# The last per-layer input of a two-layer trunk: half of its feature blocks for all tokens, half of them by halves of the tokens with weights split once

## The chip, the cores and the metric

The kernel runs on one core of a Trainium2 chip. The metric is the device time of one execution in microseconds (us), the median of several runs. A change under 0.2% (about 4.6 us here) can't be told from no change.

## The reference, cut to what matters

The trunk has two layers (DEPTH = 2) over 512 tokens of 1024 features, all in f32. What the change touches is the last step of each layer, the per-layer input embedding (PLE), in the second layer, and the final norm behind it:

```python
for i in range(DEPTH):
    ...                                   # FFN, conv + attention mixer, FFN
    gate = jax.nn.sigmoid(rmsnorm(h, ple_norm[i]) @ w_ple_gate[i])   # 1024 -> 1024
    h = h + gate * (p[i] @ w_ple_proj[i])                            # 256 -> 1024
return rmsnorm(h, final_norm)
```

`rmsnorm` divides by the root of the mean square over the 1024 features of a token, and multiplies by a gain per feature.

## The kernel before

Activations are held with features on the partitions: `h` is 8 tiles (feature blocks) of 128 features x 512 tokens. Every matrix product is made of three matmuls per 128x128 weight tile (`mm3`, lines 198 to 200): the f32 operands are split into a high part (rounded to fp32r) and a low part (the rest), and high x high, high x low and low x high are added up in PSUM.

Weights come through `Stream W`: halves of 8 tiles (128 x 1024 f32, 512 KB) are loaded by SP's DMA queue (line 51) into a pool of ten raw buffers, and `split` (lines 67 and 68) makes the high part with a copy on ACT and the low part with a subtraction on DVE, both 1024 columns wide, into rotating buffers `wh` and `wl` (four of each). `W.get` hands out the next tile. A weight that is needed twice is loaded and split twice. Other tiles of 128 x 512 come from one pool `G` of N_BIG = 58 buffers.

`ple` first splits the scaled `h` (`normed`) and `p`. A feature block m needs 8 gate tiles and 2 projection tiles, 10 x 3 matmuls. `rms` is made of two matmuls with ones (`e1ps`) and a chain on ACT and DVE: Sqrt, a reciprocal of 3.35 us, and three more DVE operations. `ple_add` then does, per block: multiply by r (line 781, DVE), Sigmoid (782, ACT), multiply by the projection (783, DVE), add to `h` (784, DVE).

In layer 0 (`halves` false) a block is one pass over 512 tokens (tiles `e0gp`, `e0pp`). In the last layer (`halves` true) all 8 blocks are done for tokens 0 to 255, then all 8 for tokens 256 to 511 (tile `e1gp`, 256 columns for the gate and 256 for the projection), and each half has an object `Final`:

- `add(k)`: square `h[k]` on ACT and add it to an accumulator on DVE (`facc`, line 259; the last two blocks stay apart as `fsq`); for the last three blocks two matmuls with a column of ones each (tile `fss`, line 808); and scale `h[k]` by the final gain on DVE (`fh`, line 811);
- `turn(kk)`: transpose four feature blocks back to tokens on the partitions, 4 transposes per 128 tokens (tile `ft`, line 819); for kk = 0 the result is copied to SBUF by ACT (`fu`, line 822);
- `finish`: the factor per token (`fr`, lines 830 to 837, with a Sqrt on ACT), four scalings (`fo`, lines 842 and 844), and four output DMAs (line 846).

The list `late` holds these steps back: up to 6 of them stay behind the blocks in the first half, 3 in the second. So the first half's `turn(0)`, `add(5)`, `add(6)` and `add(7)` are issued behind block 0 of the second half. The framework's scheduler orders the instructions of each engine at build time: the written order is the priority, and an instruction that it thinks is not ready can be passed by a later one. On the chip each engine runs its list strictly in order.

Of the kernel before, what the change touches and what calls it, by code (L numbers as in the profile page):

```python
# [24 lines left out]
SCALE = float((NOPE + ROPE) ** -0.5)  # L25
TWO_PI_PARTS = (6.28125, 0.001922607421875, 1.2695789337158203e-05, 3.958120942115784e-09, 1.0231815394945443e-11)

N_BIG = 58
N_RAW = 10
N_WH = 4  # L30

# [1 line left out]
class Stream:  # L33
# [64 lines left out]
    def halves_of(self, *tiles):  # L98

        h, l = self.get(*tiles)  # L100
        h3, l3 = (a.rearrange("p (k c) -> p k c", c=P) for a in (h, l))
        self.nc.scalar.copy(l3[:, :, :P // 2], h3[:, :, :P // 2].bitcast(F32))
        self.nc.gpsimd.memset(h3[:, :, P // 2:].bitcast(F32), 0.0)  # L103
        return l, h

    def col(self, name, l, c, rows, r0=0):

# [51 lines left out]
def trunk_kernel(ctx, tc, dims, x, p, positions, gains, rope_c, weights, out):  # L159
# [16 lines left out]
    def G(name, dt=F32):  # L176
        return gp.tile([P, S], dt, tag="g", name=name)

    def PS(name):
        return mp.tile([P, 512], F32, tag="mm", name=name)  # L180
# [21 lines left out]
    def proj(tiles, vs, name, ps=None):  # L202
        ps = PS(name) if ps is None else ps
        o = ps[:, :vs[0][0].shape[1]]
        for k, (t, v) in enumerate(zip(tiles, vs)):
            mm3(o, W.get(t), v, k == 0, k == len(tiles) - 1)
        return ps
# [30 lines left out]
    def gain(nm, l, k):  # L238
        c = col_at[nm, l] + k
        return cols[:, c:c + 1]  # L240
# [4 lines left out]
    class Squares:  # L245


        def __init__(self, name):
            self.name, self.acc = name, None

        def add(self, t):
            w = t.shape[1]
            if self.acc is None:
                self.acc = G(self.name + "acc")[:, :w]
                nc.scalar.activation(self.acc, t, AF.Square)
                return
            sq = G(self.name + "sq")[:, :w]
            nc.scalar.activation(sq, t, AF.Square)
            nc.vector.tensor_tensor(self.acc, self.acc, sq, ALU.add)
# [4 lines left out]
    def rms(acc, n, name, scale=1.0):  # L264

        ah, al = acc
        ps = PS(name + "ps")
        nc.tensor.matmul(ps, ones, ah, start=True, stop=False)
        nc.tensor.matmul(ps, ones, al, start=False, stop=True)
        r, t, ms = (rp.tile([P, S], F32, tag=g, name=name + w) for g, w in (("r", "r"), ("w", "t"), ("w", "ms")))  # L270
        nc.vector.tensor_scalar(ms, ps, 1.0 / n, EPS, ALU.mult, ALU.add)
        nc.scalar.activation(t, ms, AF.Sqrt)  # L272
        nc.vector.reciprocal(r, t)
        nc.vector.tensor_tensor(t, r, r, ALU.mult)
        nc.vector.scalar_tensor_tensor(t, t, -0.5 * scale, ms, ALU.mult, ALU.mult)
        nc.vector.scalar_tensor_tensor(r, t, 1.5 * scale, r, ALU.add, ALU.mult)
        return r
# [456 lines left out]
            nc.vector.tensor_tensor(h[m], ps, h[m], ALU.add)  # L734


    def ple(l, halves):

        name = f"e{l}"
        pt = []  # L740
        for k in range(PD // P):
            t = G(f"{name}pi{k}")
            nc.sync.dma_start(out=t, in_=p[l, k * P:(k + 1) * P, :])
            pt.append(split(t, f"{name}p{k}"))
        xs, acc = normed("ple", l, name)
        r = None
        late = []
        for toks in ((slice(0, S // 2), slice(S // 2, S)) if halves else (slice(0, S),)):
            pss = []
            final = Final(toks) if halves else None  # L750
            xt, ptt = ([(hi[:, toks], lo[:, toks]) for hi, lo in v] for v in (xs, pt))
            w = toks.stop - toks.start
            for m in range(KD):
                n = f"{m}_{toks.start}"
                pg = PS(f"{name}gp{n}")
                pp = pg[:, w:] if halves else PS(f"{name}pp{n}")
                pg = pg[:, :w]
                proj(W.col("w_ple_gate", l, m * P, D), xt, None, pg)
                proj(W.col("w_ple_proj", l, m * P, PD), ptt, None, pp)
                pss.append((pg, pp))  # L760
                if r is None and m == (2 if halves else 1):
                    r = rms(acc, D, name)
                    for mm in range(m):
                        ple_add(f"{name}{mm}_", mm, r, *pss[mm], toks)
                if r is not None:
                    ple_add(name + n, m, r, pg, pp, toks)
                if halves:
                    late.append(lambda f=final, m=m: f.add(m))
                    if m == KD // 2:
                        late.append(lambda f=final: f.turn(0))  # L770
                    if m == KD - 1:
                        late += [lambda f=final: f.turn(1), final.finish]
                    while len(late) > (3 if toks.start else 6):
                        late.pop(0)()
        for step in late:
            step()

    def ple_add(name, m, r, pg, pp, toks):
        w = toks.stop - toks.start
        g = rp.tile([P, S], F32, tag="w", name=f"{name}g{m}")[:, :w]  # L780
        nc.vector.tensor_tensor(g, pg, r[:, toks], ALU.mult)
        nc.scalar.activation(g, g, AF.Sigmoid)
        nc.vector.tensor_tensor(g, pp, g, ALU.mult)
        nc.vector.tensor_tensor(h[m][:, toks], h[m][:, toks], g, ALU.add)


    class Final:
        def __init__(self, toks):
            self.t0, self.w = toks.start, toks.stop - toks.start
            self.toks, self.nt = toks, (toks.stop - toks.start) // P  # L790
            self.sq = Squares(f"f{toks.start}")
            self.hg, self.turned = [], {}

        def add(self, k):
            n = f"{k}_{self.t0}"
            hk = h[k][:, self.toks]
            if k < KD - 2:
                self.sq.add(hk)
                sq = self.sq.acc
            else:  # L800
                sq = G("fsq" + n)
                nc.scalar.activation(sq[:, :self.w], hk, AF.Square)
            part = k - (KD - 3)
            if part == 0:
                self.ss = PS(f"fss{self.t0}")
            for t in range(self.nt if part >= 0 else 0):
                c = 4 * part + t
                nc.tensor.matmul(self.ss[:, c:c + 1], sq[:, t * P:(t + 1) * P], ones[:, 0:1].bitcast(F32),
                                 start=True, stop=True)
            hg = G("fh" + n)  # L810
            nc.vector.tensor_scalar(hg[:, :self.w], hk, gain("final", 0, k), None, ALU.mult)
            self.hg.append(hg)

        def turn(self, kk):
            for t in range(self.nt):
                n = f"{t}_{kk}_{self.t0}"
                ps = PS("ft" + n)
                for c in range(4):
                    nc.tensor.transpose(ps[:, c * P:(c + 1) * P], self.hg[4 * kk + c][:, t * P:(t + 1) * P], ident)
                if 4 * kk + 4 < KD:  # L820
                    o = G("fu" + n)
                    nc.scalar.copy(o, ps)
                    ps = o
                self.turned[t, kk] = ps

        def finish(self):
            nt = self.nt
            fr = cp.tile([P, 16], F32, tag=f"fr{self.t0}", name=f"fr{self.t0}")
            ms, rt, r, t_ = (fr[:, 4 * i:4 * i + nt] for i in range(4))
            nc.vector.tensor_scalar(ms, self.ss[:, :nt], 1.0 / D, EPS, ALU.mult, ALU.add)  # L830
            for c in (4, 8):
                nc.vector.scalar_tensor_tensor(ms, self.ss[:, c:c + nt], 1.0 / D, ms, ALU.mult, ALU.add)
            nc.scalar.activation(rt, ms, AF.Sqrt)
            nc.vector.reciprocal(r, rt)
            nc.vector.tensor_tensor(t_, r, r, ALU.mult)
            nc.vector.scalar_tensor_tensor(t_, t_, -0.5, ms, ALU.mult, ALU.mult)
            nc.vector.scalar_tensor_tensor(r, t_, 1.5, r, ALU.add, ALU.mult)
            for kk in range(KD // 4):
                for t in range(nt):
                    o = G(f"fo{self.t0}_{t}_{kk}")  # L840
                    if t % 2 == 0:
                        nc.scalar.activation(o, self.turned[t, kk], AF.Copy, scale=r[:, t:t + 1])
                    else:
                        nc.vector.tensor_scalar(o, self.turned[t, kk], r[:, t:t + 1], None, ALU.mult)
                    row = self.t0 + t * P
                    nc.sync.dma_start(out=out[row:row + P, kk * 512:(kk + 1) * 512], in_=o)

    for l in range(DEPTH):
# [52 lines left out]
```

## Time and profile before

| | us |
|---|---|
| median of 3 runs | 2320.2 (2319.61 to 2320.4) |
| the profiled execution's own time | 2319.08 |
| its span in the trace | 2317.3 |
| TensorE (PE) busy | 2294.0 (99%) |
| VectorE (DVE) busy | 1791.4 (77%) |
| ScalarE (ACT) busy | 1064.2 (46%) |

Times in rows are microseconds from the span's start, if they aren't marked ns. In a timeline row the columns are start, duration, engine, line, operation, output <- input, shapes, count, and in brackets the idle time of the engine before it with what ended it. Rows with a count above 1 merge neighbours. PEclk is the granted TensorE clock as a share of 2.4 GHz. A matmul's duration overlaps with the next one's; the step from start to start is what it costs.

### The profile page before, as it was taken

How to read it: one execution, taken by the hardware profiler on the slowest of the kernel's cores; microseconds unless marked ns; L12 is line 12 of the kernel's file. 1: busy time of each engine (PE TensorE's matmuls, PEld its weight loads, DVE VectorE, ACT ScalarE, POOL GpSimd, SP SyncE). 2: the span in 40 equal slices, each digit the busy share in tenths (PEclk: the TensorE clock that was granted, in tenths of full speed). 3: DMA queues.
4: the chain of work that ended last, by engine and by line, in shares of the span. 5: the costliest groups of instructions: out<-in, count | busy, mean ns of one | idle time of the engine just before them, and what ended most of it. 6: DMA issues, size and time to landing. Idle time of an engine off the chain costs nothing.

```text
span 2317.3 us, 33585 instructions
## 1 busy us (share of the span) xinstructions
PE 2294.0 (99%) x13696; PEld 2051.2 (89%) x13696; DVE 1791.4 (77%) x2483; ACT 1064.2 (46%) x1563; POOL 59.5 (3%) x58
## 2 busy tenths in 40 slices
PE   9999999999999999999999999999999999999997
PEld 7999988888888999998899999888888889999987
DVE  8988779745866988877898787687378679888776
ACT  7444444234544644444564444433245355444455
POOL 0000000200100000000000000001001000000000
PEclk9999999999999999999999999999999999999998
DMA  5333233332122233333223333322321213233341
GB/s 192 112 107 107 94 123 109 100 99 93 37 71 84 74 112 99 109 108 129 73 83 110 102 100 119 119 91 100 101 82 37 82 55 114 98 108 107 120 137 38
DMA packets 64523, 227.94 MB, mean 98 GB/s; under 512 B 7408, under 2 KB 7408, under 8 KB 64368
## 3 DMA queue, kind: packets, MB, share of 16 engines
q1 hardware_dynamic: 63936, 225.47, 29.7%
q8 instruction: 107, 1.75, 0.3%
q14 instruction: 48, 0.39, 0.1%
q10 hardware_dynamic: 432, 0.32, 0.0%
HBM read 223.66 MB, written 2.10 MB: 97 GB/s over the span
## 4 chain that ended last, share of the span: by engine, by line
PE 94%; DVE 4%; ACT 1%; issue 1%; DMA 0%; ACTq 0%; SPq 0%
PE a1pd L198 2%; PE b0pd L198 2%; PE b1pd L198 2%; PE a0pd L198 2%; PE b1pd L199 2%; PE b0pd L199 2%; PE a0pd L199 2%; PE a1pd L199 2%; PE a0pd L200 2%; PE a1pd L200 2%; PE b1pd L200 2%; PE b0pd L200 2%; DVE wl L68 1%; PE e1gp L198 1%; PE e1gp L199 1%; PE e1gp L200 1%
## 5 line engine op out<-in xcount | busy, mean ns | idle before, releaser
L67 ACT CAST wh<-st 128x1024 fp32r<-128x1024 f32 (+1 forms) x463 | 482.6, 1043 | 683.7 <-issue 146.3
L68 DVE TENSOR_TENSOR wl<-st,wh 128x1024 fp32r<-128x1024 f32 (+1 forms) x463 | 568.8, 1229 | 168.9 <-ACT wh L67 167.4
L67 ACT CAST wh<-s 128x1024 fp32r<-128x1024 f32 x78 | 81.9, 1050 | 101.0 <-PE b1pd L199 8.5
L68 DVE TENSOR_TENSOR wl<-s,wh 128x1024 fp32r<-128x1024 f32 x78 | 94.9, 1216 | 0.9 <-ACT wh L67 0.9
L135 DVE TENSOR_TENSOR st<-st,s 128x1024 f32<-128x1024 f32 x39 | 47.7, 1222 | 1.0
L138 DVE TENSOR_TENSOR st<-st,st 128x1024 f32<-128x1024 f32 x39 | 47.5, 1217 | 0.1
L132 DVE TENSOR_TENSOR s<-s,st 128x1024 f32<-128x1024 f32 x39 | 47.5, 1218 | 0.0
L127 DVE TENSOR_TENSOR s<-st,st 128x1024 f32<-128x1024 f32 x39 | 47.4, 1216 | 0.1
L469 DVE SCALAR_TENSOR_TENSOR h<-b0pd,h 128x512 f32<-128x512 f32 x40 | 27.5, 688 | 9.1 <-PE b0pd L200 9.1
L469 DVE SCALAR_TENSOR_TENSOR h<-b1pd,h 128x512 f32<-128x512 f32 x40 | 27.5, 688 | 9.1 <-PE b1pd L200 9.1
L469 DVE SCALAR_TENSOR_TENSOR h<-a1pd,h 128x512 f32<-128x512 f32 x40 | 27.5, 687 | 7.1 <-PE a1pd L200 7.0
L469 DVE SCALAR_TENSOR_TENSOR h<-a0pd,h 128x512 f32<-128x512 f32 x40 | 27.5, 687 | 6.4 <-PE a0pd L200 6.4
L103 POOL MEMSET wh<- 128x256 f32 x4 | 1.1, 312 | 1196.0 <-DVE wl L68 1196.0
L603 DVE TENSOR_TENSOR m1gm<-m1gmp,m1r 128x512 f32<-128x512 f32 x8 | 5.5, 691 | 26.5 <-PE m1gmp L200 26.5
L603 DVE TENSOR_TENSOR m0gm<-m0gmp,m0r 128x512 f32<-128x512 f32 x8 | 5.5, 691 | 26.2 <-PE m0gmp L200 26.2
L595 DVE TENSOR_TENSOR m1gc<-m1gcp,m1r 128x512 f32<-128x512 f32 x8 | 5.4, 689 | 11.3 <-PE m1gcp L200 11.3
L595 DVE TENSOR_TENSOR m0gc<-m0gcp,m0r 128x512 f32<-128x512 f32 x8 | 5.4, 689 | 11.3 <-PE m0gcp L200 11.3
L598 DVE TENSOR_TENSOR m0gc<-m0cop,m0gc 128x512 f32<-128x512 f32 x8 | 5.4, 690 | 8.4 <-PE m0cop L200 8.3
L598 DVE TENSOR_TENSOR m1gc<-m1cop,m1gc 128x512 f32<-128x512 f32 x8 | 5.4, 691 | 8.4 <-PE m1cop L200 8.3
L729 DVE TENSOR_TENSOR m1gm<-m1mop,m1gm 128x512 f32<-128x512 f32 x8 | 5.5, 690 | 6.6 <-PE m1mop L200 6.5
L729 DVE TENSOR_TENSOR m0gm<-m0mop,m0gm 128x512 f32<-128x512 f32 x8 | 5.5, 690 | 6.6 <-PE m0mop L200 6.5
L272 ACT ACT_TABLE_LOAD x8 | 10.3, 1283 | 0.1
(10023 smaller groups left out, 8593.3 us busy)
## 6 DMA issues: line engine op xcount, KB each, us to landing
st<-in_weights SPq DMA_DIRECT2D x416, 512.0 KB, 3.5
st<-in_weights SPq DMA_DIRECT2D x8, 256.0 KB, 5.3
h<-in_x SPq DMA_DIRECT2D x8, 256.0 KB, 5.4
out<-fo SPq DMA_DIRECT2D x8, 256.0 KB, 2.3
e0pi<-in_p SPq DMA_DIRECT2D x2, 256.0 KB, 3.7
e1pi<-in_p SPq DMA_DIRECT2D x2, 256.0 KB, 3.8
pos_i<-in_positions ACTq DMA_DIRECT2D x1, 256.0 KB, 4.4
cols<-in_gains ACTq DMA_DIRECT2D x1, 53.0 KB, 3.0
```

What stands on the lines that cost most here:

```text
L67: self.nc.scalar.copy(hi[:, w], src[:, w])
L68: self.nc.vector.tensor_tensor(lo[:, w], src[:, w], hi[:, w].bitcast(F32), ALU.subtract)
L127: tt(self.s, self.a21, self.a22, ALU.add)
L132: tt(self.s, self.s, self.a11, ALU.subtract)
L135: tt(self.a12, self.a12, self.s, ALU.subtract)
L138: tt(self.a11, self.a11, self.a21, ALU.subtract)
L198: nc.tensor.matmul(ps, wh, vh, start=first, stop=False)
L199: nc.tensor.matmul(ps, wh, vl, start=False, stop=False)
L200: nc.tensor.matmul(ps, wl, vh, start=False, stop=last)
L469: nc.vector.scalar_tensor_tensor(h[m], ps, 0.5, h[m], ALU.mult, ALU.add)
L603: nc.vector.tensor_tensor(g, ps, r, ALU.mult)
L729: nc.vector.tensor_tensor(t, mla_ps[m], t, ALU.mult)
```

## The change

In the last layer, `ple(l, last)`:

- feature blocks 0 to 3 are done for all 512 tokens at once, as layer 0 does;
- blocks 4 to 7 are done for tokens 0 to 255 and then for tokens 256 to 511, and their 40 weight tiles are loaded and split once (`W.kept`, 8 tiles at a time, in pieces of 512 columns) into 20 buffers of `G`, which stay until the end; three of the five `keep()` calls are issued with blocks 1 to 3, two with the first half's blocks 4 and 5;
- `rms` is issued behind block 1 (before: behind block 2);
- `Final` is one object for all tokens. `add` follows each `ple_add` at once, for the columns that it got; its scaling by the final gain goes from DVE to ACT. `sums`, `turn` and `finish` are calls of their own, for a half i or a block t of 128 tokens. `turn(t, 0)` of all four token blocks is issued in the first half (behind blocks 5 and 6); `sums(0, .)`, `turn(0, 1)`, `turn(1, 1)` and `finish(0)` behind blocks 4 and 5 of the second half; the rest behind the last block;
- N_BIG goes from 58 to 60, and the weight array no longer holds the last layer's PLE weights twice.

```diff
-N_BIG = 58
+N_BIG = 60
...
+    def kept(self, tiles, buffer):
+        res = []
+        st = self.raw(tiles)
+        for c in range(0, P * len(tiles), 512):
+            hi, lo = buffer(f"kh{c}", F32R), buffer(f"kl{c}", F32R)
+            self.nc.scalar.copy(hi, st[:, c:c + 512])
+            self.nc.vector.tensor_tensor(lo, st[:, c:c + 512], hi.bitcast(F32), ALU.subtract)
+            res += [(hi[:, w:w + P], lo[:, w:w + P]) for w in range(0, 512, P)]
+        return res
...
+        pss = []
+        n = (D + PD) // P
+        m0 = KD // 2 if last else KD
+        final = Final() if last else None
...
+        kept = sum((tiles(m) for m in range(m0, KD)), [])
+        ws = []
+        def keep():
+            ws.extend(W.kept([kept.pop(0) for _ in range(8)], G))
+        for m in range(m0):
+            if last and m >= 1:
+                keep()
+            pg, pp = PS(f"{name}gp{m}"), PS(f"{name}pp{m}")
+            for ps, vs, ts in ((pg, xs, tiles(m)[:KD]), (pp, pt, tiles(m)[KD:])):
+                proj(ts, vs, None, ps)
+            pss.append((pg, pp))
+            if m == 1:
+                r = rms(acc, D, name)
+                ple_add(f"{name}0_", 0, r, *pss[0], slice(0, S))
+                if last:
+                    final.add(0, slice(0, S))
+            if m >= 1:
+                ple_add(name, m, r, pg, pp, slice(0, S))
+                if last:
+                    final.add(m, slice(0, S))
...
+        for i in range(2):
+            toks = slice(i * (S // 2), (i + 1) * (S // 2))
+            for m in range(m0, KD):
+                if kept:
+                    keep()
+                ps = PS(f"{name}gp{m}_{i}")
+                pg, pp = ps[:, :S // 2], ps[:, S // 2:]
+                for j, (hi, lo) in enumerate(xs + pt):
+                    o, first, end = (pg, j == 0, j == KD - 1) if j < KD else (pp, j == KD, j == n - 1)
+                    mm3(o, ws[(m - m0) * n + j], (hi[:, toks], lo[:, toks]), first, end)
+                ple_add(f"{name}{i}", m, r, pg, pp, toks)
+                final.add(m, toks)
+                if i == 0 and m - m0 in (1, 2):
+                    for t in (0, 1) if m - m0 == 1 else (2, 3):
+                        final.turn(t, 0)
+                if i == 1 and m == m0:
+                    final.sums(0, KD - 3)
+                if i == 1 and m == m0 + 1:
+                    final.sums(0, KD - 2)
+                    final.sums(0, KD - 1)
+                    final.turn(0, 1)
+                    final.turn(1, 1)
+                    final.finish(0)
+        final.sums(1, KD - 3)
+        final.sums(1, KD - 2)
+        final.turn(2, 1)
+        final.sums(1, KD - 1)
+        final.turn(3, 1)
+        final.finish(1)
...
+        def add(self, k, toks):
+            hk = h[k][:, toks]
+            if k == 0:
+                nc.scalar.activation(self.acc[:, toks], hk, AF.Square)
             else:
-                sq = G("fsq" + n)
-                nc.scalar.activation(sq[:, :self.w], hk, AF.Square)
+                sq = self.sq[k, toks.start * 2 // S] = G(f"fsq{k}")[:, :hk.shape[1]]
+                nc.scalar.activation(sq, hk, AF.Square)
+                if k < KD - 2:
+                    nc.vector.tensor_tensor(self.acc[:, toks], self.acc[:, toks], sq, ALU.add)
+            nc.scalar.mul(self.hg[k][:, toks], hk, gain("final", 0, k))
...
-            nc.vector.tensor_scalar(hg[:, :self.w], hk, gain("final", 0, k), None, ALU.mult)
...
-    n_tiles = (sum(ins[n].size for n in _WEIGHTS) + DEPTH * D * ROPE
-               + ins["w_ple_gate"][-1].size + ins["w_ple_proj"][-1].size) // (P * P)
+    n_tiles = (sum(ins[n].size for n in _WEIGHTS) + DEPTH * D * ROPE) // (P * P)
```

## Rows read from the trace of the kernel before

**Rows 1.** The page: the span, and the busy time of each engine.

```profile
span 2317.3 us, 33585 instructions
PE 2294.0 (99%) x13696; PEld 2051.2 (89%) x13696; DVE 1791.4 (77%) x2483; ACT 1064.2 (46%) x1563; POOL 59.5 (3%) x58
```

**Rows 2.** All waits of PE over the span, longest in total first: who waited for whom, us in total, times, longest.

```profile
PE a0pg L198 <- ACT a0x0h L193: 5.3, 1, 5.3
PE fss L808 <- DVE f0acc L259: 2.6, 1, 2.6
PE fss L808 <- DVE f256acc L259: 1.9, 1, 1.9
PE ft L819 <- DVE fh L811: 1.8, 2, 1.6
```

**Rows 3.** Windows of the stage: stretch, length, then busy us of each engine, the granted clock (PEclk), the DMA share and GB/s.

```profile
2264.00:2285.00 21.00, 16.54 (x102) 15.83 (x101) 15.82 (x41) 9.51 (x19) 0.00 (x0) 0.76 0.00 1
2306.00:2318.00 12.00, 3.14 (x25) 2.50 (x22) 4.20 (x16) 5.18 (x10) 0.00 (x0) 0.68 0.23 88
```

**Rows 4.** Timeline of PE: the first matmul of the last PLE, and then from the start of block 0 of the second half until its regular course again.

```profile
2234.71 0.28 PE L198 MATMUL e1gp<-e1x0h,wh 128*128 128x256 f32 x1
...
2264.22 0.28 PE L198 MATMUL e1gp<-e1x0h,wh 128*128 128x256 f32 x1
...
2267.82 0.60 PE L819 MATMUL ft<-ident,fh 128*128 128x128 f32 x4
...
2273.76 1.01 PE L808 MATMUL fss<-ones,f0acc 128*128 128x1 f32 x4 [2.62 <-DVE f0acc L259]
2274.63 0.56 PE L198 MATMUL e1gp<-e1x0h,wh 128*128 128x256 f32 x1
...
2282.89 1.11 PE L819 MATMUL ft<-ident,fh 128*128 128x128 f32 x8
2283.75 0.36 PE L198 MATMUL e1gp<-e1x0h,wh 128*128 128x256 f32 x1
```

**Rows 5.** Windows of PE alone in that stretch: stretch, length, busy, granted clock, DMA share, GB/s.

```profile
2270.00:2272.00 2.00, 0.44 (x2) 1.00 0.00 0
2272.00:2274.00 2.00, 0.24 (x2) 0.70 0.00 0
2274.00:2276.00 2.00, 2.00 (x10) 0.50 0.00 0
```

**Rows 6.** Timeline of DVE around it: the end of the rms chain (L276), the first and the last `ple_add` of the first half, and the scaling of its fourth block (L811).

```profile
2257.93 0.69 DVE L276 SCALAR_TENSOR_TENSOR e1r<-e1t,e1r 128x512 f32<-128x512 f32 x1
...
2262.02 0.75 DVE L784 TENSOR_TENSOR h<-h,e_g 128x256 f32<-128x256 f32 x2
...
2270.30 0.34 DVE L811 TENSOR_SCALAR fh<-h,cols 128x256 f32<-128x256 f32 x1
2270.56 0.41 DVE L784 TENSOR_TENSOR h<-h,e_0g 128x256 f32<-128x256 f32 x1
```

**Rows 7.** Timeline of PE in layer 0's PLE, which is done for 512 tokens at once: the first matmul of its blocks 0 and 1, and the rms matmul behind block 1.

```profile
1093.33 0.39 PE L198 MATMUL e0gp<-e0x0h,wh 128*128 128x512 f32 x1
...
1100.13 0.39 PE L198 MATMUL e0gp<-e0x0h,wh 128*128 128x512 f32 x1
...
1106.93 0.40 PE L268 MATMUL e0ps<-e0ah,ones 128*128 128x512 f32 x1
```

**Rows 8.** Timeline of DVE in layer 0's PLE: a weight split before the rms chain with the idle time ahead of it, the chain's end, the split and the first multiplication behind it, and the last addition of blocks 2 and 3.

```profile
1105.31 1.22 DVE L68 TENSOR_TENSOR wl<-st,wh 128x1024 fp32r<-128x1024 f32 x1 [4.21 <-ACT wh L67]
...
1114.77 0.69 DVE L276 SCALAR_TENSOR_TENSOR e0r<-e0t,e0r 128x512 f32<-128x512 f32 x1
1116.69 1.23 DVE L68 TENSOR_TENSOR wl<-st,wh 128x1024 fp32r<-128x1024 f32 x1 [1.23 <-ACT wh L67]
1117.83 0.68 DVE L781 TENSOR_TENSOR e_g<-e0gp,e0r 128x512 f32<-128x512 f32 x1
...
1126.49 1.28 DVE L784 TENSOR_TENSOR h<-h,e_0g 128x512 f32<-128x512 f32 x2
```

**Rows 9.** Timeline of ACT, single durations: a scaling by a column of gains and a Square over 512 columns, and a Square over 256.

```profile
2225.34 0.71 ACT L193 ACTIVATE e1x3h<-h,cols 128x512 fp32r<-128x512 f32 x1
2225.96 0.62 ACT L258 ACTIVATE e1sq<-h 128x512 f32<-128x512 f32 x1
...
2291.20 0.40 ACT L258 ACTIVATE f256sq<-h 128x256 f32<-128x256 f32 x1
```

**Rows 10.** Timelines of PE, DVE and ACT behind the last block of the kernel, each engine's rows in order of time.

```profile
2305.42 1.03 PE L819 MATMUL ft<-ident,fh 128*128 128x128 f32 x8
2308.39 0.61 PE L808 MATMUL fss<-ones,f256acc 128*128 128x1 f32 x4 [1.94 <-DVE f256acc L259]
...
2305.62 0.42 DVE L781 TENSOR_TENSOR e_256g<-e1gp,e1r 128x256 f32<-128x256 f32 x1 [1.81 <-PE e1gp L200]
2307.59 0.42 DVE L784 TENSOR_TENSOR h<-h,e_256g 128x256 f32<-128x256 f32 x1
...
2306.05 0.58 ACT L822 COPY fu<-ft 128x512 f32<-128x512 f32 x1 [3.16 <-PE ft L819]
2308.47 1.28 ACT L833 ACT_TABLE_LOAD   x1
2310.79 0.20 ACT L833 ACTIVATE fr<-fr 128x2 f32<-128x2 f32 x1 [1.03 <-DVE fr L832]
2311.62 0.16 DVE L837 SCALAR_TENSOR_TENSOR fr<-fr 128x2 f32<-128x2 f32 x1
```

More of the change, by code (lines that the diff above doesn't have):

```diff
@@ L734, in mixer, with ple @@
             nc.vector.tensor_tensor(h[m], ps, h[m], ALU.add)
-    def ple(l, halves):
+    def ple(l, last):
         name = f"e{l}"
@@ L745, in ple @@
         xs, acc = normed("ple", l, name)
[L746 to L774, printed above, removed]
@@ L775, in ple, with tiles @@
-        for step in late:
-            step()
+        pss = []
+        n = (D + PD) // P
+        m0 = KD // 2 if last else KD
+        final = Final() if last else None
+        def tiles(m):
+            return W.col("w_ple_gate", l, m * P, D) + W.col("w_ple_proj", l, m * P, PD)
+        kept = sum((tiles(m) for m in range(m0, KD)), [])
[18 more added lines that the diff above has]
+                    final.add(m, slice(0, S))
@@ new lines, in ple @@
+        if not last:
+            return
+        for i in range(2):
[21 more added lines that the diff above has]
+                    final.finish(0)
@@ L787, in trunk_kernel, with __init__ @@
     class Final:
[L788 to L799, printed above, removed]
-            else:
-                sq = G("fsq" + n)
-                nc.scalar.activation(sq[:, :self.w], hk, AF.Square)
+        def __init__(self):
+            self.acc, self.ss, self.sq, self.turned = G("facc"), {}, {}, {}
+            self.hg = [G(f"fh{k}") for k in range(KD)]
@@ L803, in add, with sums @@
+        def sums(self, i, k):
             part = k - (KD - 3)
             if part == 0:
-                self.ss = PS(f"fss{self.t0}")
-            for t in range(self.nt if part >= 0 else 0):
+                self.ss[i] = PS(f"fss{i}")
+            sq = self.sq[k, i] if part else self.acc[:, i * (S // 2):(i + 1) * (S // 2)]
+            for t in range(2):
                 c = 4 * part + t
-                nc.tensor.matmul(self.ss[:, c:c + 1], sq[:, t * P:(t + 1) * P], ones[:, 0:1].bitcast(F32),
+                nc.tensor.matmul(self.ss[i][:, c:c + 1], sq[:, t * P:(t + 1) * P], ones[:, 0:1].bitcast(F32),
@@ L809, in add @@
                                  start=True, stop=True)
-            hg = G("fh" + n)
-            nc.vector.tensor_scalar(hg[:, :self.w], hk, gain("final", 0, k), None, ALU.mult)
[L812 to L830, printed above, removed]
+        def turn(self, t, kk):
+            n = f"{t}_{kk}"
+            ps = PS("ft" + n)
+            for c in range(4):
+                nc.tensor.transpose(ps[:, c * P:(c + 1) * P], self.hg[4 * kk + c][:, t * P:(t + 1) * P], ident)
+            if 4 * kk + 4 < KD:
+                o = G("fu" + n)
+                nc.scalar.copy(o, ps)
+                ps = o
+            self.turned[t, kk] = ps
@@ L831, in finish @@
+        def finish(self, i):
+            nt = NT // 2
+            fr = cp.tile([P, 16], F32, tag=f"fr{i}", name=f"fr{i}")
+            ms, rt, r, t_ = (fr[:, 4 * j:4 * j + nt] for j in range(4))
+            ss = self.ss[i]
+            nc.vector.tensor_scalar(ms, ss[:, :nt], 1.0 / D, EPS, ALU.mult, ALU.add)
             for c in (4, 8):
-                nc.vector.scalar_tensor_tensor(ms, self.ss[:, c:c + nt], 1.0 / D, ms, ALU.mult, ALU.add)
+                nc.vector.scalar_tensor_tensor(ms, ss[:, c:c + nt], 1.0 / D, ms, ALU.mult, ALU.add)
@@ L839, in finish @@
                 for t in range(nt):
-                    o = G(f"fo{self.t0}_{t}_{kk}")
+                    o = G(f"fo{i}_{t}_{kk}")
+                    src = self.turned[i * nt + t, kk]
                     if t % 2 == 0:
-                        nc.scalar.activation(o, self.turned[t, kk], AF.Copy, scale=r[:, t:t + 1])
+                        nc.scalar.activation(o, src, AF.Copy, scale=r[:, t:t + 1])
                     else:
-                        nc.vector.tensor_scalar(o, self.turned[t, kk], r[:, t:t + 1], None, ALU.mult)
-                    row = self.t0 + t * P
+                        nc.vector.tensor_scalar(o, src, r[:, t:t + 1], None, ALU.mult)
+                    row = (i * nt + t) * P
                     nc.sync.dma_start(out=out[row:row + P, kk * 512:(kk + 1) * 512], in_=o)
```

## The prediction, made before the change was run

> **What bounds the kernel now.** I read the page first: PE is busy for 2294.0 of 2317.3 us [rows 1]. So a change pays where it shortens PE's own work, takes a wait of PE away, or shortens the stretches at both ends where PE can't work. The list of PE's waits comes next: after the wait for the first input, the three longest all belong to the final norm, 2.6, 1.9 and 1.8 us [rows 2]; the 1.9 us lie behind the last block, in the tail, the other 4.4 us in the middle of the last PLE. The windows show what else is there: between 2264 and 2285 PE is busy for 16.54 of 21 us and its mean granted clock is 0.76 [rows 3].
>
> The timeline of that stretch tells the story. PE ends block 0 of the second half at 2267.82 and turns to the first half's transposes and sums. These need `fh` and `f0acc` from DVE. DVE could start with the additions only when r was there, at 2258.6, had to do all eight blocks of the half in one go (first addition 2262.02, last 2270.56), and made the scaling of the fourth block, which the first transposes need, only at 2270.30 [rows 6]. PE waits; the clock is still 1.00 from 2270 to 2272, falls in the next two microseconds, and is 0.50 from 2274 on, 1.2 GHz of 2.4 [rows 5]. So block 1, from 2274.63 to 2282.89, runs at half speed too, and only at 2283.75 does PE take up its course again [rows 4].
>
> The last thing to read is the tail: the last block's matmuls make room at 2305.42, and the span ends 11.9 us later, a chain of small steps on DVE, ACT and PE and the output DMAs [rows 1, 10].
>
> **Term 1: four blocks for all tokens.** A block over 256 tokens takes 30 matmuls from 2264.22 to 2267.82: 0.1200 us each [rows 4]. A block over 512 tokens takes 30 matmuls in 6.80 us: 0.2267 us each [rows 7]. Two halves cost 0.2400, so each of 120 pairs saves 0.0133 us: **-1.6 us**. This is pure PE time on a bound engine, so it moves the end by as much.
>
> The Trainium skill's page "TensorE: Matmul & The Clock Gate", section "Back-to-back issue gap", would make this nearly nothing: it gives a step of N/2.4 ns plus 2.5 ns for an isolated matmul, so halving N costs only the extra 2.5 ns, an estimate of 0.3 us for 120 pairs, and the sum below would be 1.3 us less. The rows' step of 0.1200 us at 256 columns is longer than the page's 0.109, and a step measured in this kernel decides.
>
> **Term 2: the stall in the middle.** From 2267.82 to 2283.75 are 15.93 us [rows 4]. The work in it is one block (30 x 0.1200 = 3.6), 16 transposes (8 of them take 2282.89 to 2283.75, 0.86, so 1.7), and three groups of small sums (a group of four takes 0.61 or less at the end of the kernel [rows 10], so up to 1.8): 7.1 us at full clock. The rest, **-8.8 us**, is waiting and half clock. It goes if the transposes and sums find their inputs ready and the clock stays. The sums of the first half are moved to a place two blocks later; the transposes of blocks 0 to 3 come after two half blocks.
>
> **Term 3: what can wait instead.** The first call that can stall is `turn(0, 0)`, which needs the scaled block 3. PE gets there at 2234.7 (its first PLE matmul [rows 4]) + 120 x 0.2267 + 0.5 (the two rms matmuls) + 60 x 0.1200 = 2269.6. When is block 3 ready? Layer 0 is the template, with the same blocks and the same rms: from its first matmul at 1093.33 to the last addition of blocks 2 and 3 at 1127.77 are 34.4 us [rows 7, 8]. That gives 2269.1 here. To this come three additions to `facc` on DVE (0.6 each) and a scaling of 0.71 on ACT [rows 9], and from it goes the split at 1116.69 with the 1.23 us of idling before it [rows 8], since the whole blocks now need five halves of weights and not ten. So 2269 to 2271.6, and a wait of 0 to 2.0 us; I take **+0.7**, nearer to the low end, because the first additions are what gets earlier. The upper bound of this term is the removed stall itself, 8.8, if the clock falls again.
>
> **Term 4: transposes that come ahead of the last block.** Before, eight of the second half's transposes ran behind the last block, beside the tail's chain [rows 10]. Now they run before it: 8 x 0.11 = **+0.9** on PE.
>
> **Term 5: the tail.** Before, r per token (`fr`) is ready at 2311.78, 6.4 us after 2305.42 [rows 10]; what follows (four scalings, four DMAs) is the same in both. In the chain, the copy of `fu` on ACT at 2306.05 stands ahead of the last Sigmoid, the last addition is done at 2308.01, and the sums of three blocks come after it. After: multiplication, Sigmoid, multiplication, addition in a row, each 0.42 with 0.05 between, ready 2.0 after the last matmul; Square 0.40, then the scaling on ACT (0.40 plus the 0.09 by which a scaling by a column is dearer at 512 columns [rows 9]) beside the last sums, 0.85 together; then the table load for Sqrt, 1.28, which had been hidden and is now in line; then 1.0 from Sqrt to `fr`, as 2310.79 to 2311.78 [rows 10]. With handoffs 5.2 us: **-1.2**. Bounds: -2.0 if the load hides again, and +1.5 if the first half's output scalings and a second table load stand ahead of the last Sigmoid on ACT.
>
> The Trainium skill's page "ScalarE: Activation LUTs", section "Rules for kernel authors", says to put multiplications on VectorE rather than ScalarE, which speaks against moving the final gain to ACT: on DVE it would run beside the Square, and the table load could start some 0.4 us earlier. By that rule the sum would stand 0.4 us lower with the scaling left where it was; no run here shows it yet.
>
> **What costs nothing.** The 40 kept tiles need 10 pieces of 512 columns on ACT and DVE in place of 10 whole splits for the repeated half (1.22 us each on DVE [rows 8]): less work. DVE idles in layer 0 for 4.21 us ahead of one split and has further gaps before r; the ten pieces (0.6 each, half a split) fill such gaps. Without that cover they would stand in DVE's way after r, 6 us in all, and delay block 3 by as much. SP's queue gets ten loads fewer, and its outputs of the first half come when nothing else loads: DMA moves 1 GB/s between 2264 and 2285 [rows 3]. The two more G buffers leave the stages before as they are; I allow 1 us either way for a different order there.
>
> **Sum:** -1.6 - 8.8 + 0.7 + 0.9 - 1.2 = **-10.0 us**. The profiled execution took 2319.1, 1.8 more than its span; that gives 2309.1. The median of the runs lies 1.1 above that execution, so I predict **2310.2 us**, 0.43% faster.
>
> **Rivals.** A change under 0.2%, 4.6 us, would not be told from none.
>
> *B, the stall moves and stays.* PE's `turn(0, 0)` or the sums find DVE late, wait for 4 us or more, and the clock falls to 1.2 GHz for a block or two. For it: DVE's work behind r is the same kind, and the scheduler misjudged just this before. Against it: DVE has four big blocks where it had eight small ones behind r, the scalings go to ACT, and layer 0's timetable ends within 2 us of PE's arrival. It gives back most of term 2, 5 to 9 us: 2315 to 2319.
>
> *C, slower: the kept weights come late.* If ACT's and DVE's ten pieces are queued behind the chain that waits for r (or wait for G buffers, of which 20 are held), the first half block finds no weights at 2262.4. With all of DVE's additions first, the first pieces would be done at about 2272: PE idle for 10 us, and then the half clock over some 10 us of work, 5 more. That is +15 against the forecast, 2325, slower by 0.2%. It decides from a wait of about 10 us up. Against it: the pieces need only a load and a free buffer, both there before r, and ACT has gaps of several microseconds beside each split.
>
> *D, the change works and gives more.* The tail hides the load too and nothing waits: 0.8 and 0.7 more, about 2308.7.
>
> **How the numbers follow.** The forecast with its own range, 2306 to 2314, gets 0.78 (D in it); B 0.16; C 0.04; an unknown upset upstream 0.02. The range takes in the bounds of terms 3 and 5 and the nearer part of B: 2306 to 2316. Faster by over 0.2% means below 2315.6: the forecast and a small part of B, 0.82. Within 0.2%: most of B, 0.14. Slower: C and what is unknown, 0.04.
>
> **What would show it.** Right: matmul steps of 0.227 in four blocks of `e1gp`, ten fewer weight splits, PE without a wait above 2 us before the last block, clock 1.00 until then, last block done near 2296, and the Sqrt's table load on the chain of the tail, `fr` ready some 5.2 us after the last matmul. Wrong: a long wait of `ft` or `fss` with a granted clock of 0.5 behind it (B), a wait of `e1gp` for the kept pieces (C), or a tail above 12 us.

## The result, and the profile after

The changed kernel takes **2308.7 us** (median of 6 runs, 2307.74 to 2309.11), the kernel before 2320.3 (6 runs, 2319.41 to 2320.65). The ratio is 0.995, with a 95% interval of 0.9938 to 0.9963. 11.6 us are gone; 2310.2 was predicted, with a range from 2306 to 2316.

The page of the kernel after, span and busy time of each engine, answers to [rows 1]:

```profile
span 2306.9 us, 33263 instructions
PE 2287.3 (99%) x13576; PEld 2040.5 (88%) x13576; DVE 1776.3 (77%) x2447; ACT 1059.3 (46%) x1562; POOL 59.2 (3%) x58
```

The profiled execution took 2308.72. Between the two profiled executions the gain is 10.4, since that of before lies 1.2 below its median. PE has 6.7 us less of busy time in a span that is 10.4 shorter.

PE's waits in the kernel after (who for whom, us in total, times, longest), against [rows 2]:

```profile
PE a0pg L209 <- ACT a0x0h L204: 5.6, 1, 5.6
PE fss L854 <- ACT fsq L841: 0.9, 1, 0.9
```

The 4.4 us of waits in the middle of the last PLE are gone and none has come in their place. The only wait of the final norm is the 0.9 in the tail, where 1.9 was. The window of the stage (stretch, length, busy us of PE, PEld, DVE, ACT and POOL, granted clock, DMA share, GB/s), against [rows 3]:

```profile
2264.00:2285.00 21.00, 21.00 (x179) 21.00 (x179) 14.93 (x32) 14.56 (x32) 0.00 (x0) 1.00 0.00 1
```

PE is busy for all of the 21 us (16.54 before), at a granted clock of 1.00 (0.76 before). The timeline of PE, against [rows 4], shows the marks of the stage: the first matmul of the last PLE, the first of the halved blocks, the transposes that were moved, the first sums of the first half, the last matmul, and the sums behind it:

```profile
2235.79 0.39 PE L209 MATMUL e1gp<-e1x0h,wh 128*128 128x512 f32 x1
...
2263.48 0.28 PE L209 MATMUL e1gp<-e1x0h,kh 128*128 128x256 f32 x1
...
2269.24 0.82 PE L861 MATMUL ft<-ident,fh 128*128 128x128 f32 x6
2269.81 0.36 PE L209 MATMUL e1gp<-e1x6h,kh 128*128 128x256 f32 x1
...
2271.80 0.38 PE L861 MATMUL ft<-ident,fh 128*128 128x128 f32 x2
...
2275.12 1.04 PE L861 MATMUL ft<-ident,fh 128*128 128x128 f32 x8
2275.91 0.36 PE L209 MATMUL e1gp<-e1x0h,kh 128*128 128x256 f32 x1
...
2283.18 0.50 PE L854 MATMUL fss<-ones,facc 128*128 128x1 f32 x4
2283.55 0.36 PE L209 MATMUL e1gp<-e1x0h,kh 128*128 128x256 f32 x1
...
2296.01 0.28 PE L211 MATMUL e1gp<-e1p1h,kl 128*128 128x256 f32 x1
2296.14 0.50 PE L854 MATMUL fss<-ones,facc 128*128 128x1 f32 x4
```

In the kernel before, the last matmul of the stage starts here:

```profile
2305.29 0.29 PE L200 MATMUL e1gp<-e1p1h,wl 128*128 128x256 f32 x1
```

From first to last matmul the stage took 70.58 us (2234.71 in [rows 4] to 2305.29) and takes 60.22 (2235.79 to 2296.01): **-10.36**. This stage length is the figure by which the experiments are compared below, since the start of the stage itself moves by a microsecond or more between executions (2234.31 to 2236.03 in the profiles of this study).

Last, the tail of the kernel after, ACT and DVE apart, each in order of time, against [rows 10]:

```profile
2296.79 0.42 ACT L825 ACTIVATE e11g<-e11g 128x256 f32<-128x256 f32 x1 [1.05 <-DVE e11g L824]
2298.16 0.42 ACT L841 ACTIVATE fsq<-h 128x256 f32<-128x256 f32 x1 [0.95 <-DVE h L827]
2298.48 0.49 ACT L844 ACTIVATE fh<-h,cols 128x256 f32<-128x256 f32 x1
2298.99 1.28 ACT L876 ACT_TABLE_LOAD   x1
2300.29 0.20 ACT L876 ACTIVATE fr<-fr 128x2 f32<-128x2 f32 x1
...
2297.70 0.42 DVE L827 TENSOR_TENSOR h<-h,e11g 128x256 f32<-128x256 f32 x1
2301.11 0.16 DVE L880 SCALAR_TENSOR_TENSOR fr<-fr 128x2 f32<-128x2 f32 x1
```

The Sigmoid no longer stands behind a copy, and Square, scaling, table load and Sqrt follow one another without a gap. `fr` is ready at 2301.27, 5.1 us after PE turned from the blocks to the sums at 2296.14, where it was 6.4.

### The profile page after: what moved, and what is told of

Read it like the earlier page. It is cut to its first block, busy times and chain, and to the rows that moved or that the text cites. A ratio compares the mean times of both kernels' runs of the same rounds, so it can differ in the third digit from the quotient of the medians.

```text
span 2306.9 us, 33263 instructions
## 1 busy us (share of the span) xinstructions
PE 2287.3 (99%) x13576; PEld 2040.5 (88%) x13576; DVE 1776.3 (77%) x2447; ACT 1059.3 (46%) x1562; POOL 59.2 (3%) x58
## 4 chain that ended last, share of the span: by engine, by line
PE 95%; DVE 3%; ACT 1%; issue 1%; DMA 0%; ACTq 0%; SPq 0%
PE a0pd L209 2%; PE a1pd L209 2%; PE b0pd L209 2%; PE b1pd L209 2%; PE a1pd L210 2%; PE b1pd L210 2%; PE b0pd L210 2%; PE a0pd L210 2%; PE b1pd L211 2%; PE b0pd L211 2%; PE a0pd L211 2%; PE a1pd L211 2%; DVE wl L68 1%; PE e1gp L209 1%; PE e1gp L211 1%; PE e1gp L210 1%
## 5 line engine op out<-in xcount | busy, mean ns | idle before, releaser
L67 ACT CAST wh<-st 128x1024 fp32r<-128x1024 f32 (+1 forms) x448 | 467.1, 1043 | 663.9 <-issue 135.7
L68 DVE TENSOR_TENSOR wl<-st,wh 128x1024 fp32r<-128x1024 f32 (+1 forms) x448 | 550.7, 1229 | 162.4 <-ACT wh L67 161.0
```

Source lines behind the costliest of these rows:

```text
L67: self.nc.scalar.copy(hi[:, w], src[:, w])
L68: self.nc.vector.tensor_tensor(lo[:, w], src[:, w], hi[:, w].bitcast(F32), ALU.subtract)
```

## The experiments

The theory: most of the gain is the stall in the middle, and it goes because the transposes and sums find their inputs ready; the whole blocks and the tail give the rest. The rival explanation: what counts is that the weights are loaded and split once, which unloads DVE and ACT. Times below are medians, beside the kernel before on the same chip in the same session; "from the change" means an edit made to the changed kernel.

**The stall alone.** The kernel before, with the steps in `late` held back longer, and nothing else of the change:

```diff
-                    while len(late) > (3 if toks.start else 6):
+                    while len(late) > (6 if not toks.start else 99 if m < 2 else 5 if m == 2 else 3):
```

> The kernel before, with nothing changed but the place of the first half's transposes and sums: they are issued behind block 2 of the second half, two blocks (7.2 us) later, so that DVE's additions, which ended at 2273.7, are done when PE comes to them at about 2275. All weights are still loaded and split twice, all blocks still run by halves. Theory (the stall and the half clock were only a matter of when PE came to these instructions): the 8.8 us of term 2 go and nothing else changes, 2320.3 - 8.8 = about 2311.5, clock 1.00 through the stage. Rival (the stall comes of the double work of splitting, and goes only with the kept weights and the whole blocks): the wait moves with the instructions, 2317 to 2320.

Measured: 2312.45 against 2319.54, ratio 0.9969 (0.9958 to 0.9981): -7.1. The stage takes 63.48 us. Its longest wait inside the stage, and the window of [rows 3]:

```profile
PE e1gp L200 <- DVE wl L68: 2.0, 1, 2.0
```

```profile
2264.00:2285.00 21.00, 19.05 (x162) 18.81 (x161) 19.15 (x48) 14.12 (x27) 0.00 (x0) 1.00 0.00 1
```

The clock stays at 1.00. PE waits 2.0 us for a weight split: DVE is busy for 19.15 of 21 us, and the split that PE needs starts only at 2272.65, behind a row of small operations, most of them for the first half's blocks. So the stall with its half clock is worth some 9 us (7.1 and 2.0), and the wait, which the expectation of 2311.5 had left out, took part of it. A change of one line in the order of issue is worth most of the whole change.

**Four blocks as pairs of halves.** From the change: blocks 0 to 3 are done for 256 tokens and then for the other 256, with the same split weight tiles, so only the matmul's width differs:

```diff
-                proj(ts, vs, None, ps)
+                wt = [W.get(t) for t in ts]
+                for at in (slice(0, S // 2), slice(S // 2, S)):
+                    for k, (hi, lo) in enumerate(vs):
+                        mm3(ps[:, at], wt[k], (hi[:, at], lo[:, at]), k == 0, k == len(vs) - 1)
```

(for the last layer alone)

> The changed kernel (2308.7), with blocks 0 to 3 computed as pairs of matmuls over 256 tokens with the same weight tiles, in place of one over 512; all else the same. By the rows of before (0.1200 us a step at 256 columns, 0.2267 at 512) 120 pairs cost 1.6 us more: 2310.3. By the page's 2.5 ns a matmul, 0.3 us: 2309.0.

Measured: 2309.98 against 2319.54, 0.996 (0.9945 to 0.9975). First and last matmul of the stage:

```profile
2235.00 0.28 PE L209 MATMUL e1gp<-e1x0h,wh 128*128 128x256 f32 x1
...
2297.06 0.28 PE L211 MATMUL e1gp<-e1p1h,kl 128*128 128x256 f32 x1
```

62.06 us, 1.84 more than in the changed kernel. The median is 1.3 above that of the change, but the two come from different sessions, so the stage is the better measure.

**Nothing kept.** From the change: the weights of blocks 4 to 7 are loaded and split again for the second half, as before the change:

```diff
-                    mm3(o, ws[(m - m0) * n + j], (hi[:, toks], lo[:, toks]), first, end)
+                    mm3(o, W.get(ts[j]), (hi[:, toks], lo[:, toks]), first, end)
```

(with `ts = tiles(m)` ahead of it, no `keep()` calls, and these weights twice in the weight array)

> The changed kernel, but blocks 4 to 7 load and split their weights again for the second half of the tokens, through the stream, as the kernel before did; nothing is kept. Theory (the kept weights are worth nothing on their own, PE is bound and the splits lie under it): within 1 us of 2308.7. Rival (the saved splitting is what keeps DVE ahead of PE): a wait of transposes or sums on DVE comes back, 2312 to 2318.

Measured: 2308.5 against 2319.54, 0.9953 (0.9937 to 0.997). The window:

```profile
2264.00:2285.00 21.00, 21.00 (x179) 21.00 (x178) 20.02 (x34) 18.19 (x33) 0.00 (x0) 1.00 0.01 1
```

DVE is busy for 20.02 of 21 us instead of 14.93, ACT for 18.19 instead of 14.56, and PE waits for neither: the stage takes 60.23. The kept weights by themselves are worth nothing here, and as far as they go the rival explanation falls. The run puts back only half of the saved splits, since the whole blocks still split theirs once; with all of them, in the order-only kernel above, one split made PE wait for 2.0 us. The order at build time moved too: the first eight transposes come in three groups, the last at 2272.60, so a later `fh` need not show as a wait.

**The kept pieces late.** From the change: all five `keep()` calls are written behind block 3. This makes the third rival (C) happen on purpose.

```diff
-            if last and m >= 1:
-                keep()
...
         if not last:
             return
+        while kept:
+            keep()
```

> The changed kernel, but all five calls that split the kept weights are issued behind block 3. This is rival C put to the test: DVE then does all additions of blocks 0 to 3 first, and the first pieces come at about 2270 where PE wants them at 2263.5. If the price of C was right: PE waits 6 to 7 us, the clock falls to 0.5 for about 10 us, 2308.7 + 11 = about 2320. If the pieces find another place or the cover is wider than that: within 2 us of 2308.7.

Measured: 2315.91 against 2319.54, 0.9985 (0.9975 to 0.9994), +7.2 from the change. The wait that is new in the stage, and the windows of PE alone from its start on (stretch, length, busy, granted clock, DMA share, GB/s), and ACT's first pieces:

```profile
PE e1gp L209 <- ACT kh L112: 5.8, 1, 5.8
```

```profile
2264.00:2266.00 2.00, 0.00 (x0) 1.00 0.00 0
2266.00:2268.00 2.00, 0.00 (x0) 0.68 0.00 0
2268.00:2270.00 2.00, 0.71 (x2) 0.50 0.01 4
2270.00:2272.00 2.00, 2.00 (x10) 0.50 0.00 0
2272.00:2274.00 2.00, 2.00 (x13) 0.61 0.00 0
2274.00:2276.00 2.00, 2.00 (x19) 1.00 0.00 0
```

```profile
2268.63 2.69 ACT L112 CAST kh<-st 128x512 fp32r<-128x512 f32 x5
```

ACT does the `fh` and `fsq` of the whole blocks first and starts with the pieces only at 2268.63. The stage takes 68.35 us, 8.1 more than in the changed kernel: the wait of 5.8, and 2.3 that go with the half clock. C's mechanism is real, with a smaller price than the prediction's, where the wait was 10 and the half clock 5; the expectation's 2320, with a half clock of about 10 us, was too high as well. Even so, by the medians, nearly two thirds of the gain are gone.

**The rms one block later.** From the change: `rms` behind block 2, where the kernel before had it.

```diff
-            if m == 1:
+            m_r = 2 if last else 1
+            if m == m_r:
                 r = rms(acc, D, name)
```

(the blocks before it are added up behind it, as in the changed kernel)

> The changed kernel, with the rms matmuls and what hangs on them one block (6.8 us) later, behind block 2 as the kernel before had them. Theory (what made the old stall was that DVE got r late for the first transposes): block 3's scaling, at 2270.8 in the changed kernel, comes at 2275 to 2277, PE is at the first transposes by 2270.5 and waits 4 to 5 us for them, and some of the half clock comes back: 2313 to 2318. Rival (with whole blocks DVE has room enough, the place of rms does not matter): within 1 us of 2308.7.

Measured: 2316.41 against 2320.02, 0.9985 (0.9975 to 0.9995), +7.7 from the change. Waits, and windows of PE as above:

```profile
PE ft L863 <- ACT fh L846: 3.3, 1, 3.3
PE e1gp L209 <- DVE e_g L826: 0.9, 1, 0.9
```

```profile
2272.00:2274.00 2.00, 0.00 (x0) 0.99 0.00 0
2274.00:2276.00 2.00, 1.15 (x4) 0.50 0.02 4
...
2278.00:2280.00 2.00, 2.00 (x11) 0.50 0.00 0
2280.00:2282.00 2.00, 2.00 (x16) 0.80 0.04 8
```

This is rival B, made to happen. The chain that gives r ends on DVE (L287) 7 us later than in the changed kernel:

```profile
2263.33 0.69 DVE L287 SCALAR_TENSOR_TENSOR e1r<-e1t,e1r 128x512 f32<-128x512 f32 x1
```

```profile
2256.28 0.69 DVE L287 SCALAR_TENSOR_TENSOR e1r<-e1t,e1r 128x512 f32<-128x512 f32 x1
```

(first this kernel, then the changed one). The third block is then scaled only at 2274.10 to 2274.80, and the two transposes that need it wait:

```profile
2274.10 0.70 ACT L846 ACTIVATE fh<-h,cols 128x512 f32<-128x512 f32 x1
```

The fourth, for which the expectation had looked, is scaled from 2276.58 to 2277.29; the order had put its two transposes at 2278.39, and they don't wait. The stage takes 68.14 us, 7.9 more: 4.2 of waits, and 3.7 that go with the half clock. So the place of `rms` decides whether the stall is gone or only moved. From the end of r to PE's first transposes are 9.2 us in the kernel before (2258.62 to 2267.82), 6.6 here (2264.02 to 2270.66), and 12.3 in the changed kernel (2256.97 to 2269.24): the two that leave less time are the two that stall. Whether `rms` one block earlier would have cured the kernel before by itself was not run.

**All pieces early.** From the change: all five `keep()` calls ahead of block 1.

```diff
-            if last and m >= 1:
+            while last and m == 1 and kept:
                 keep()
```

> The changed kernel, with all five calls that split the kept weights issued before block 1, so that their ten pieces fall into DVE's idle 6.5 us ahead of the rms chain, which is where the prediction had put them. Theory (PE waits for nothing in this stage, so DVE's time is free): within 0.5 us of 2308.7. Rival (DVE's fuller load behind r does cost PE something): 1 us less or more.

Measured: 2308.68 against 2320.02, 0.9953 (0.9938 to 0.9968). Where the pieces are now done, and the window:

```profile
2243.34 4.30 DVE L113 TENSOR_TENSOR kl<-st,kh 128x512 fp32r<-128x512 f32 x7
```

```profile
2264.00:2285.00 21.00, 21.00 (x179) 21.00 (x178) 10.74 (x23) 10.26 (x24) 0.00 (x0) 1.00 0.00 1
```

Seven pieces stand in one row in the gap before r, DVE does 4.19 us less in the window, and the stage is the same, 60.25. The margin on DVE buys nothing, as the reload took nothing.

**The gain of the final norm on DVE.** From the change:

```diff
-            nc.scalar.mul(self.hg[k][:, toks], hk, gain("final", 0, k))
+            nc.vector.tensor_scalar(self.hg[k][:, toks], hk, gain("final", 0, k), None, ALU.mult)
```

> The changed kernel, with the final gain applied on DVE again (before: DVE, after: ACT). Theory (the tail's chain runs over the Square, the scaling and the table load on ACT, so the scaling's 0.4 us are in line): 0.4 us less, 2308.3. Rival (the sums on PE end as late as the table load, or DVE's additions are delayed by eight more operations): no gain, or up to 1 us more.

Measured: 2308.68 against 2320.02, 0.9952 (0.9937 to 0.9967). The last matmul, the table load and the last operation of `fr`:

```profile
2295.34 0.28 PE L211 MATMUL e1gp<-e1p1h,kl 128*128 128x256 f32 x1
...
2297.92 1.28 ACT L876 ACT_TABLE_LOAD   x1
...
2300.04 0.16 DVE L880 SCALAR_TENSOR_TENSOR fr<-fr 128x2 f32<-128x2 f32 x1
```

From the last matmul to the last operation are 4.70 us, where the changed kernel takes 5.10 (2296.01 to 2301.11): -0.4, seen in the trace and too small for the medians. The stage takes 60.36, 0.14 more, with no wait of PE in it: the scaling's move from DVE to ACT, which the prediction put down against rival B, is not what keeps the stall away.

**The pool at its old size.** From the change:

```diff
-N_BIG = 60
+N_BIG = 58
```

> The changed kernel with the old pool of 58 buffers. In the profile of the changed kernel the last PLE starts 1.1 us later than before (2235.8 for 2234.7); 0.3 of it is the first input's load, the rest comes up in the heads of both mixers, where only the pool's size is different. Theory (the larger pool changes DVE's order there): that 0.8 us comes back, 2307.9, and the last PLE still fits. Rival (the shift is chance of one execution): 2308.7 and the same starts.

Measured: 2308.11 against 2320.02, 0.995 (0.9935 to 0.9965). Two waits of the changed kernel far ahead of the last PLE are gone with it, 0.4 us together:

```profile
PE m0t20t L694 <- DVE m0h3qn0l L202: 0.2, 1, 0.2
PE m1t20t L694 <- DVE m1h3qn0l L202: 0.2, 1, 0.2
```

The stage starts at 2234.31, 1.48 earlier than in the changed kernel's profile. That is not all the pool's: over all profiles of this study the stage starts at 2234.98 to 2236.03 with 60 buffers (eight kernels) and at 2234.31 to 2235.22 with 58 (five, that of before among them), and these overlap. The medians by themselves don't resolve 0.4.

**Put together, and one block more.** In one session ran the changed kernel again, the three small edits together (pool of 58, gain on DVE, pieces early), and these with five whole blocks in place of four:

```diff
-        m0 = KD // 2 if last else KD
+        m0 = KD // 2 + 1 if last else KD
...
-                if i == 0 and m - m0 in (1, 2):
-                    for t in (0, 1) if m - m0 == 1 else (2, 3):
+                if i == 0 and m - m0 in (0, 1):
+                    for t in (0, 1) if m == m0 else (2, 3):
                         final.turn(t, 0)
```

(30 kept tiles, and the first half's sums, transposes and output all behind the second half's first block)

> The changed kernel itself, beside the others on one chip: 2308.7 if the chip doesn't matter.

> The changed kernel with three edits of the runs so far together: the final gain on DVE (tail's chain 5.1 to 4.7 us from the last matmul to the factors), the pool of 58 (two waits of 0.2 us in the heads gone), and the kept weights split ahead of block 1. Theory (these add up): 0.8 us below the changed kernel in the same call, about 0.03%. Rival: within the spread of the runs, 0.3 us.

> The combined kernel with five whole blocks in place of four, three by halves, 30 tiles kept, and the first half's norm behind block 5 of the second half. Theory (a whole block saves 30 x 0.0133 us of PE, and the first half's norm still ends before the last block): 0.4 us below the combined kernel, 1.2 below the changed one. Rival (the first half's norm comes too near to the tail, its two table loads and four scalings delay the last Sigmoids): as the combined kernel or 1 us above it.

Measured, against 2319.76 for the kernel before:

| | median (lowest to highest of 5) | ratio (95%) | stage |
|---|---|---|---|
| the changed kernel again | 2308.24 (2308.17 to 2308.99) | 0.9952 (0.9938 to 0.9966) | 60.23 |
| three edits | 2307.49 (2306.91 to 2308.23) | 0.9949 (0.9934 to 0.9963) | 60.25 |
| three edits, five whole blocks | 2307.30 (2306.83 to 2307.62) | 0.9947 (0.9934 to 0.996) | 59.85 |

The three edits together give 0.75 of the 0.8 us that were expected. All of the last one's runs lie below all of the changed kernel's, by 0.9 us in the median, where 1.2 were expected. That is the fastest kernel of this study, and the step is under the 0.2% that the metric tells from nothing. Its stage is 0.4 shorter, as 30 pairs of matmuls at 0.0133 would give.

## Why the prediction was right, step by step

| term | predicted | measured | from |
|---|---|---|---|
| 1, whole blocks | -1.6 | -1.8 | stage with the pairs of halves |
| 2, stall | -8.8 | -9.3 | what terms 1, 3 and 4 leave of the stage's -10.36 |
| 3, new wait | +0.7 | 0 | PE's waits in the stage: none |
| 4, transposes | +0.9 | +0.8 | 2275.12 to 2275.91 for eight |
| 5, tail | -1.2 | -1.2 | 6.36 (2305.42 to 2311.78) to 5.13 (2296.14 to 2301.27) |

**Term 1** held: 1.84 for 120 pairs is 0.0153 each, where 0.0133 came from the steps. The Trainium skill, "TensorE: Matmul & The Clock Gate", section "Back-to-back issue gap", would have made it 0.3 by its step for an isolated matmul; the experiment with pairs of halves shows that the measured step was the right one to use here.

**Term 2** had the right mechanism and was 0.5 small. The likely cause is the size of the work that I left in the stall: I put the three groups of small sums at 0.61 each, an upper bound from a row in the tail. In the changed kernel a group costs 0.37 (2283.18 to 2283.55), 0.7 less for three, which is more than enough. The order-only experiment supports the size from the other side: -7.1 in spite of a new wait of 2.0.

**Term 3** was the likeliest term to go wrong, and its mechanism held, with one piece of luck. The fourth whole block's last addition ends at 2269.21, where 2269.1 was forecast; but the stage began 1.08 us later than I had put it. Counted from the stage's first matmul, the addition ends after 33.4 us, where layer 0 had given 34.4. Its scaling on ACT ends at 2270.84, after 35.1 (forecast 34.3 to 36.9):

```profile
2268.52 0.69 DVE L827 TENSOR_TENSOR h<-h,e1g 128x512 f32<-128x512 f32 x1
...
2270.13 0.71 ACT L844 ACTIVATE fh<-h,cols 128x512 f32<-128x512 f32 x1
```

In the written order PE would have come to `turn(0, 0)` behind block 5, 34.9 us after its first matmul as forecast, which is 2270.7 here; so a wait of up to 0.2 was due, the low end of the forecast's 0 to 2.0, and not the 0.7 that I took. Even that did not come: the scheduler had put the six transposes of the first three blocks ahead of block 5's last 12 matmuls, at 2269.24, and the last two only at 2271.80, behind some matmuls of block 6, when their input had been there for 1 us. An order made at build time can take such a wait away. Before the change it had not: PE stood behind the late `fh`.

**Terms 4 and 5** came out as worked out, to 0.1 us. The tail's chain has the predicted steps: the scaling on ACT took 0.49 (0.40 plus 0.09 was put), and the table load of 1.28 stands on the chain. The rule of the Trainium skill's "ScalarE: Activation LUTs", section "Rules for kernel authors", that a multiplication belongs on VectorE, agrees with the trace here: moved back to DVE, the tail is 0.40 shorter.

**What costs nothing: the claim held, the reason did not.** I said that the ten kept pieces would fill DVE's gaps before r. They did not. On DVE, the two pieces that came early, the idle time ahead of the rms chain, the first of the pieces behind r, and the last:

```profile
2240.68 1.29 DVE L113 TENSOR_TENSOR kl<-st,kh 128x512 fp32r<-128x512 f32 x2
2250.05 0.69 DVE L282 TENSOR_SCALAR e1ms<-e1ps 128x512 f32<-128x512 f32 x1 [6.50 <-PE e1ps L280]
...
2264.58 0.69 DVE L113 TENSOR_TENSOR kl<-st,kh 128x512 fp32r<-128x512 f32 x1 [0.43 <-ACT kh L112]
...
2275.66 0.68 DVE L113 TENSOR_TENSOR kl<-st,kh 128x512 fp32r<-128x512 f32 x1
```

Eight of ten came behind r, among the additions, while DVE had idled for 6.50 us before it. The prediction said that without such cover they would delay block 3 by 6 us. They did not, since only two of the eight (2264.58 and 2265.79) came ahead of the fourth block's last addition. That they came no later than they did is what counted: with all of them written behind block 3 the price was 7.2 us, and with all of them ahead of r there was nothing to gain.

**What the sum left out.** The sum of stage and tail, -11.6, is the difference of the medians, but the two traces differ by 10.4 only: the changed kernel's profiled execution entered the stage 1.08 later than that of before. That the sum fits the medians is chance in part, since the profiled execution of before was 1.2 faster than its median and the changed kernel's was not. Of the 1.08, 0.4 are two waits that come with the larger pool, as the run at 58 shows; the cause of the rest was not found, and the starts of the other kernels differ by as much. The forecast's "1 us either way" covered it.

**The rivals.** B did not occur, but it was close: r 7 us later brings it, at 2316.4, inside the 2315 to 2319 that I gave it. C did not occur; provoked, it costs +7.2 and not +15, and ends 0.15% below the kernel before, not above it. I had sized both its wait (10 for 5.8) and the half clock (5 for some 2 us) too high. D came half true: nothing waits, its 0.7, but the table load stayed on the chain, its 0.8. That its time, 2308.7, came out to the digit is luck: the other 0.8 came from terms 1, 2 and 4.

**What stays open.** How the 0.75 us of the three edits together divide among pool, gain and pieces is not settled: the trace shows 0.4 each for the first two, and the medians of the single edits don't resolve them.

## What to carry to other kernels

Where the bound engine runs its list in order, ask for each of its side steps (a transpose, a sum, a conversion) when its input is ready, and give the distance from the source of the lateness, here r, to that step. Moving the steps back in the order of issue gained 7.1 us here, and putting the source one block later lost 7.7 of the whole change's 11.6. Loading and splitting the kept weights once in place of twice gained nothing, though with all weights split twice (the order-only kernel) one split made PE wait for 2.0 us. A timetable taken from a twin stage in the same trace (layer 0 here) was good to 1 us in 34, if it is counted from the stage's own start.

## What was unexpected of the hardware

After a gap PE resumed at half clock (1.2 of 2.4 GHz), and how long it stayed there was not the same each time. The windows show when the granted clock fell and rose, as a window's mean lies between the two levels. In the kernel before it fell in the window from 2272 [rows 5] and rose in this one:

```profile
2282.00:2284.00 2.00, 2.00 (x16) 0.74 0.04 8
```

From the means the fall is at 2272.8 and the rise at 2283.0. PE resumed at 2273.76 [rows 4], so it worked at half clock for some 9.3 us. In the kernel with r later, after a gap of 3.3 us that ends at 2274.86, the clock fell at 2274.0 and rose at 2280.8: 5.9 us of work at half clock. In the one with the pieces late, after a gap of 5.8 us that ends at 2269.29, it fell at 2266.7 and rose at 2273.6: 4.3 us. So the longest gap had the shortest half clock behind it. Counted from the fall, the clock was low for 6.8 us in both of these and for 10.2 in the kernel before; in the longest gap more of that time lay in the waiting. Why it was longer in the kernel before was not tried. A gap of 2.0 us (the order-only kernel) left the clock at 1.00. For a forecast: the stalls of 3 to 6 us seen here cost 2 to 5 us of PE's time beside the waits themselves (2.3 and 3.7 in the two experiments, and 9.3 less 4.4 of waits in the kernel before).
